# Attention of a decoder block on one core: q, k, probabilities and values from float32r pairs to float16 pairs, with wider spacing of the attention steps

## The chip, the cores and the metric

The kernel runs on one core of one Trainium2 chip. The metric is the device time of one execution in microseconds (us), from the launch on the device to its end; shorter is better. Times are medians over several executions.

The engines are named as in the profile: PE is TensorE (matrix products; PEld its weight loads), DVE is VectorE, ACT is ScalarE, POOL is GpSimd, SP is SyncE, whose queue issues most of the DMAs.

## The reference

One decoder block over 1024 tokens of width 1024. Attention and a causal convolution work on the same normalised input, are merged by sigmoid gates and projected; a SwiGLU feed-forward layer follows. The part that matters here is attention: three groups of 8 heads of width 64, with dilation 1, 4 and 16, each query attending at most 128 steps back, with a learned bias by distance.

```python
s = jnp.einsum('brnqhd,brnkhd->brnhqk', qb, kb).astype(jnp.float32) * (Dh ** -0.5) + bias
s = jnp.where(valid[:, None], s, NEG_INF)
lse = jax.nn.logsumexp(s, axis=-1)
p = jnp.exp(s - lse[..., None])
o = jnp.einsum('brnqhk,brnkhd->brnqhd', p, vb.astype(jnp.float32))
...
alpha = jax.nn.softmax(jnp.stack(lses, axis=0), axis=0)
o = jnp.einsum('gbsh,gbshd->bshd', alpha, jnp.stack(outs, axis=0))
```

All arrays are float32. The group outputs are merged with weights that come from their softmax denominators.

## The kernel before

**Products in two parts.** A float32 operand is carried as a high part in a short format and a low part that holds the rest. A product of two such operands is three products: high by high, high by low, low by high. Most of the kernel uses float16 parts, after a scaling of the weights by a power of two that is taken from their size (`self.scale`); attention, the output projections and the last layer use float32r parts.

**Stages.** In order: the first gate and convolution inputs; the remaining gates, convolution inputs and then q and k, in pairs of weight tiles by a Winograd scheme of seven products (`winograd`, lines 454 to 456), with the depthwise convolution on VectorE beside it; the value projection V (`v`, lines 1094 to 1098: products of 256 columns), with attention beside it; the gate and convolution-output units (`unit`, lines 438 to 442: products of 512 columns), into which attention runs on; the attention output, the mix projection and the feed-forward layer.

**q and k.** `qk_pair` writes each result to DRAM in two parts (`d_qk`), rows grouped by dilation. `stack_load` later brings them back for one pair of heads: `k` with its high rows over its low rows, and q as two tiles whose second halves GpSimd fills by copies (`double`, lines 1035 and 1036). So a score takes two products of full height (line 1192).

**Attention steps.** `attention` is a generator of 96 steps: 12 head pairs of 8 query blocks each. A step has one key block or two. At step s it emits: the scores of block s and, on VectorE, their sum with the bias and the row bound (`att_s`, lines 1192 and 1195); the exponential of block s - 1 on ScalarE (`att_e`, 1205); the transposes of block s - 3 and their two parts, the cast on ScalarE and the subtraction on VectorE (`att_t`, 1228, 1233, 1234); the products with the values of block s - 4, one of 128 and one of 64 columns per head and key block (`att_p`, 1249 and 1251), and a sum of their parts (1256). Loads for the next head pair are issued at its first steps, the bias tile (`bias_tile`, 613) as the fifth.

**Values.** Each V eviction (ScalarE, 1104 and 1106) writes float32 to DRAM (`d_v`); `values` loads a pair's values, and `value_parts` makes two parts of them on ScalarE and GpSimd (1069 and 1070) just before use.

**What sets the order.** All instructions are recorded in the order in which the Python code emits them, and each engine works through its own in that order. The generator is advanced by `beat`: each product of the V stage and of the units adds `RATE` to a credit (`RV` in the V stage, `RU` behind it), and a whole credit runs the generator to its next `yield`, three or four to a step. Other side work (`tick`, `later`, `bg`) hangs on counts of products too. So the numbers `RV` and `RU` say how many large products stand between two pieces of attention. Tiles come from rings of buffers (`half`: 11 tiles of 128x512 float32, named c; `slot`: b; `ring`: d), and whoever takes a buffer waits for its last reader.

Of the kernel before, what the change touches and what calls it, by code (L numbers as in the profile page):

```python
# [18 lines left out]
T = 1024  # L19
# [16 lines left out]
RV, RU = 0.42, 0.8  # L36
# [6 lines left out]
TINY, W_TOP, H_TOP = 2.0 ** -60, 2.0 ** -13, 256.0  # L43

# [25 lines left out]
class Build:  # L70
# [21 lines left out]
    def ring(self):  # L92
        self.uid += 1
        return self.pool.tile([128, 1024], F32, tag="d", bufs=NRING, name=f"d{self.uid}")
# [680 lines left out]
    def conv_consts(self):  # L775

        nc = self.nc
        self.nbu = self.small.tile([128, 8], F32, name="nbu")
# [169 lines left out]
    def qk_pair(self, g, hp, job):  # L948
# [3 lines left out]
        _, un, _, un8 = self.scale[job]  # L952
        dil = DILS[g]
# [17 lines left out]
        def parts(y, hf, dst, scale):  # L971
            h = self.half(F32R)
            nc.scalar.activation(h, y, AF.Copy, scale=scale)
            nc.vector.scalar_tensor_tensor(y.bitcast(F32R), y, scale, f(h), op0=OP.mult, op1=OP.subtract)

            def store():
                out(dst, 0, hf, f(h))
                out(dst, 1, hf, y)

            self.hold(store)  # L980

        def row1(hf):
            def g(z, x):
                y = self.half()
                nc.vector.tensor_tensor(perm(y), nat(z), nat(x), op=OP.add)
                return lambda: parts(y, hf, dk, un)
            return g

        def f22(x, v):
            y = self.half()  # L990
            nc.vector.tensor_tensor(perm(y), nat(x), nat(v), op=OP.add)
            return lambda: parts(y, 1, dq, un8)

        def f21(x):
            h, l = self.half(F32R), self.half(F32R)
            nc.scalar.activation(perm(h), nat(x), AF.Copy, scale=un8)
            nc.vector.scalar_tensor_tensor(perm(l), nat(x), un8, perm(f(h)), op0=OP.mult, op1=OP.subtract)

            def store():
                out(dq, 0, 0, f(h))  # L1000
                out(dq, 1, 0, f(l))

            self.hold(store)
# [8 lines left out]
    def stack_load(self, p, i):  # L1012
# [4 lines left out]
        if i < 2:  # L1017
            a, b = self.slot(F32R), self.slot(F32R)
            nc.sync.dma_start(f(a[top]), dq[i * 64:i * 64 + 64])
            nc.sync.dma_start(f(b[low]), dq[128 + i * 64:192 + i * 64])  # L1020
            p[2][i][1:] = a, b
        elif i < 4:
            k = self.slot(F32R)
            for part, rows in enumerate((top, low)):
                e = part * 128 + (i - 2) * 64
                nc.sync.dma_start(f(k[rows]), dk[e:e + 64])
# [4 lines left out]
    def double(self, p, hf):  # L1031

        s, top, low = slice(hf * H, (hf + 1) * H), slice(0, 64), slice(64, 128)
        for k, a, b in p[2]:
            self.nc.gpsimd.tensor_copy(a[low, s], f(a[top, s]))
            self.nc.gpsimd.tensor_copy(b[top, s], f(b[low, s]))
# [13 lines left out]
    def values(self, g, hp):  # L1050

        x = self.slot()
# [11 lines left out]
    def value_parts(self, x, i):  # L1064

# [1076 lines left out]
```

## Time and profile before

| | us |
|---|---|
| median of 3 runs | 1684.94 (1684.65 to 1686.24) |
| the profiled execution: its own time | 1684.47 |
| the profiled execution: span of its instructions | 1682.6 |
| TensorE busy in the span | 1644.7 |
| VectorE, ScalarE, GpSimd busy | 1275.8, 995.4, 468.0 |
| attention, first score to last product with values | 599 to 849 of the span |
| end of the V products | 782 |

In the profile a row of a group has the line, the engine, the operation, out<-in by the program's tile names, the shape and count, then busy us and the mean ns of one, then idle time before it and what ended it. In a timeline a row has start and duration in us. In windows a row has the busy us of each engine in a stretch of time, with the number of instructions, then the TensorE clock that was granted (1.00 is full), the share of the DMA engines and GB/s. In a list of waits a row has the total us, the number of times and the longest.

### The profile page before, as it was taken

Reading aid. Unit: us, or ns where it says so; the run is one execution under the profiler, and the core shown is the slowest. Engines: PE = TensorE matmul, PEld = TensorE weight load, DVE = VectorE, ACT = ScalarE, POOL = GpSimd, SP = SyncE. Lnnn points to the kernel's source line nnn. Section 1 sums busy time; section 2 is a strip of 40 time slices with the busy share of each in tenths; the row PEclk is TensorE's granted clock in tenths of the full one; section 3 lists DMA queues with packets and bytes.
Section 4 is the critical chain, followed back from the end, with each engine's and each line's share of the span. In section 5 each row is a group of like instructions: output and inputs, shape, how many; then the busy total and the mean of one; then the engine's idle time right before and its main releaser. Section 6 shows DMA issues by size and latency. Waiting matters only on the chain.

```text
span 1682.6 us, 25027 instructions
## 1 busy us (share of the span) xinstructions
PE 1644.7 (98%) x8757; PEld 1060.7 (63%) x8757; DVE 1275.8 (76%) x2467; ACT 995.4 (59%) x1875; POOL 468.0 (28%) x384
## 2 busy tenths in 40 slices
PE   8999999999999989999999999999999999999998
PEld 6744444444444979989788878544444444588886
DVE  6889999999998766697764856677667657677686
ACT  6476676666665777778622456755555555454453
POOL 0007777787775145646300110000000000000000
PEclk9999999999999999999999999999999999999999
DMA  4352343455567897978845732222322322494334
GB/s 168 126 191 88 125 150 132 149 185 198 175 172 202 246 278 219 248 206 250 267 175 190 278 112 72 75 107 102 138 99 94 130 96 94 154 377 126 107 126 156
DMA packets 159481, 277.06 MB, mean 165 GB/s; under 512 B 46993, under 2 KB 78412, under 8 KB 159356
## 3 DMA queue, kind: packets, MB, share of 16 engines
q1 hardware_dynamic: 155148, 263.30, 47.2%
q0 software_dynamic: 3920, 11.91, 2.3%
q8 instruction: 69, 1.13, 0.3%
q14 instruction: 56, 0.46, 0.1%
q10 hardware_dynamic: 288, 0.27, 0.0%
HBM read 184.81 MB, written 95.33 MB: 166 GB/s over the span
## 4 chain that ended last, share of the span: by engine, by line
PE 77%; DVE 9%; ACT 4%; POOL 3%; issue 3%; DMA 2%; DVEq 0%; SPq 0%; POOLq 0%; ACTq 0%
PE p L2026 12%; PE p L454 11%; PE p L456 11%; PE p L455 11%; PE p L1751 4%; PE p L438 4%; PE p L442 4%; PE p L440 4%; DVE p L833 3%; PE p L692 2%; PE p L1098 2%; PE p L1094 2%; PE p L1096 2%; PE p L1192 2%; PE p L1228 1%
## 5 line engine op out<-in xcount | busy, mean ns | idle before, releaser
L456 PE MATMUL p<-b,b 128*128 128x512 f16 x1032 | 391.1, 379 | 2.9 <-POOL b L294 2.9
L454 PE MATMUL p<-b,b 128*128 128x512 f16 x1032 | 391.0, 379 | 2.2 <-ACT c L468 1.6
L455 PE MATMUL p<-b,b 128*128 128x512 f16 x1032 | 391.0, 379 | 0.0
L2026 PE MATMUL p<-b,b 128*128 128x512 f32 x924 | 209.8, 389 | 0.0
L2026 PEld LDWEIGHTS p<-b,b 128*128 128x128 f32 x924 | 173.4, 188 | 36.1
L456 PEld LDWEIGHTS <-b 128*128 128x128 f16 x1032 | 100.8, 98 | 127.6 <-POOL b L294 6.6
L454 PEld LDWEIGHTS <-b 128*128 128x128 f16 x1032 | 100.9, 98 | 120.9
L455 PEld LDWEIGHTS <-b 128*128 128x128 f16 x1032 | 100.8, 98 | 119.5 <-issue 3.0
L833 DVE SCALAR_TENSOR_TENSOR p<-b,par,p 128x511 f32<-128x511 f32 (+14 forms) x232 | 163.9, 739 | 0.0
L438 PE MATMUL p<-b,b 128*128 128x512 f32 (+1 forms) x368 | 144.8, 393 | 1.5 <-ACT b L284 1.5
L442 PE MATMUL p<-b,b 128*128 128x512 f32 (+1 forms) x368 | 143.9, 391 | 0.4 <-DVE b L285 0.4
L440 PE MATMUL p<-b,b 128*128 128x512 f32 (+1 forms) x368 | 143.9, 391 | 0.0
L285 DVE SCALAR_TENSOR_TENSOR b<-d,sc,b 128x1024 f16<-128x1024 f32 x40 | 51.2, 1281 | 87.7 <-ACT b L284 87.7
L294 POOL TENSOR_TENSOR b<-d,b 128x1024 f16<-128x1024 f32 x44 | 96.1, 2184 | 74.7 <-ACT b L293 74.6
L1094 PE MATMUL p<-b,b 128*128 128x256 f16 x384 | 105.9, 276 | 0.1
L1096 PE MATMUL p<-b,b 128*128 128x256 f16 x384 | 106.0, 276 | 0.0
L1098 PE MATMUL p<-b,b 128*128 128x256 f16 x384 | 105.9, 276 | 0.0
L1344 DVE TENSOR_TENSOR b<-c,b 128x512 fp32r<-128x512 f32 (+1 forms) x101 | 70.1, 695 | 37.1 <-ACT b L1343 37.0
L1343 ACT CAST b<-b 128x512 fp32r<-128x512 f32 (+1 forms) x117 | 72.1, 617 | 42.9 <-PE p L2026 18.3
L1344 DVE TENSOR_TENSOR b<-b,b 128x512 fp32r<-128x512 f32 (+1 forms) x117 | 80.1, 688 | 19.7 <-ACT b L1343 18.2
L1751 PE MATMUL p<-b,b 128*128 128x512 f32 x384 | 90.1, 392 | 0.0
L1205 ACT ACTIVATE c<-c,stat 128x128 f32<-128x128 f32 (+1 forms) x192 | 84.8, 445 | 8.8 <-DVE stat L1195 8.7
(272 smaller groups left out, 3548.9 us busy)
## 6 DMA issues: line engine op xcount, KB each, us to landing
b<-w_in SPq DMA_DIRECT2D x30, 512.0 KB, 4.6
dk<-c SPq DMA_DIRECT2D x48, 256.0 KB, 2.5
dq<-c SPq DMA_DIRECT2D x48, 256.0 KB, 3.1
b<-dq SPq DMA_DIRECT2D x48, 256.0 KB, 8.6
b<-dk SPq DMA_DIRECT2D x48, 256.0 KB, 8.6
b<-w_fi SPq DMA_DIRECT2D x24, 512.0 KB, 5.2
d<-w_in SPq DMA_DIRECT2D x23, 512.0 KB, 4.8
dqS<-c SPq DMA_DIRECT2D x44, 256.0 KB, 2.0
```

What stands on the lines that cost most here:

```text
L438: nc.tensor.matmul(ps, hi[:, s], a, start=kt == 0, stop=False)
L440: nc.tensor.matmul(ps, hi[:, s], b, start=False, stop=False)
L442: nc.tensor.matmul(ps, lo[:, s], a, start=False, stop=kt == nk - 1)
L454: nc.tensor.matmul(ps, hi[:, s], a, start=first and kt == 0, stop=False, skip_group_check=True)
L455: nc.tensor.matmul(ps, hi[:, s], b, start=False, stop=False, skip_group_check=True)
L456: nc.tensor.matmul(ps, lo[:, s], a, start=False, stop=kt == 3, skip_group_check=True)
L833: nc.vector.scalar_tensor_tensor(A[i][:, j:], src[i][:, :H - j], w[i], A[i][:, j:], op0=OP.mult, op1=OP.add)
L1094: nc.tensor.matmul(o, a, hi[:, s], start=kt == 0, stop=False)
L1096: nc.tensor.matmul(o, a, lo[:, s], start=False, stop=False)
L1344: nc.vector.tensor_tensor(s[:, 512:512 + n], src, f(s[:, :n]), op=OP.subtract)
L1751: nc.tensor.matmul(banks[tt][nh], st, wt[:, nh * H:(nh + 1) * H], start=bool(kt == 0 and a), stop=bool(kt == KT - 1 and b))
L2026: nc.tensor.matmul(acc[t], x, y, start=first and e == 0, stop=last and e == 2, skip_group_check=True)
```

## The change

The attention operands become float16 pairs.

- `qk_pair` scales each q and k by `KEEP`, a fixed power of two, and writes high and low float16 parts; the factor that undoes it, with the weights' scale, is kept per head pair (`sig`) and multiplied in where scores and bias are added. For that the bias tile is divided by the same factor: `scale_bias`, a reciprocal on VectorE and a pass of ScalarE over the bias tile, emitted behind the seventh step of the pair before. `d_qk` is float16, so its stores and loads have half the bytes. Two operand tiles share one slot (`packed`).
- V evictions write the high part (ScalarE) and the low part (VectorE) directly, as float16 under `KEEP`; `d_v` holds both parts, with the same number of bytes as before. `value_parts` is gone: the loaded tile is used as it is.
- The probabilities' two parts are float16 under `P_TOP`, in one tile instead of two. The factors of values and probabilities are undone in the merge (`vun`).
- `RV` goes from 0.42 to 0.36, `RU` from 0.8 to 0.66.

```diff
-RV, RU = 0.42, 0.8
+RV, RU = 0.36, 0.66
...
+KEEP, P_TOP = 2.0 ** -12, 2.0 ** 14
...
-        def parts(y, hf, dst, scale):
-            h = self.half(F32R)
-            nc.scalar.activation(h, y, AF.Copy, scale=scale)
-            nc.vector.scalar_tensor_tensor(y.bitcast(F32R), y, scale, f(h), op0=OP.mult, op1=OP.subtract)
...
+        def parts(y, hf, dst):
+            x = self.half(F16, [128, T])
+            nc.scalar.activation(x[:, :H], y, AF.Copy, scale=KEEP)
+            nc.vector.scalar_tensor_tensor(x[:, H:], y, KEEP, x[:, :H], op0=OP.mult, op1=OP.subtract)
+            store(hf, dst, x)
...
-            a, b = self.slot(F32R), self.slot(F32R)
-            nc.sync.dma_start(f(a[top]), dq[i * 64:i * 64 + 64])
-            nc.sync.dma_start(f(b[low]), dq[128 + i * 64:192 + i * 64])
+            a, b = self.packed(), self.packed()
+            nc.sync.dma_start(a[top], dq[i * 64:i * 64 + 64])
+            nc.sync.dma_start(b[low], dq[128 + i * 64:192 + i * 64])
...
+    def scale_bias(self, p):
+        c = 4 * p[0] + p[1]
+        r = self.tiny(1, "rsig", 3)
+        self.nc.vector.reciprocal(r, self.sig[:, c:c + 1])
+        self.nc.scalar.activation(p[3], p[3], AF.Copy, scale=r)
...
-    def value_parts(self, x, i):
-
-        v = self.slot(F32R)
-        d = v.rearrange("p (t e c) -> p t e c", t=8, e=2)
-        y = x[:, i * H:(i + 1) * H].rearrange("p (t c) -> p t c", t=8)
-        self.nc.scalar.copy(d[:, :, 0], y)
-        self.nc.gpsimd.tensor_tensor(d[:, :, 1], y, f(d[:, :, 0]), op=OP.subtract)
-        return v
...
             if i % 4 == 0:
-                x = self.ring()
-                nc.scalar.activation(x[:, :H], ps, AF.Copy, scale=un)
-            else:
-                nc.scalar.activation(x[:, H:], ps, AF.Copy, scale=un)
+                x = self.ring(F16, [128, 2 * T])
+            y = x[:, i % 4 * H:i % 4 * H + T].rearrange("p (a e c) -> p a e c", e=2, c=64)
+            z = ps.rearrange("p (a c) -> p a c", c=64)
+            nc.scalar.activation(y[:, :, 0], z, AF.Copy, scale=KEEP)
+            nc.vector.scalar_tensor_tensor(y[:, :, 1], z, KEEP, y[:, :, 0], op0=OP.mult, op1=OP.subtract)
+            if i % 4:
                 self.later(2, lambda i=i, x=x: out(i, x))
                 x = None
...
+                if u == 7 and nxt:
+                    self.scale_bias(nxt)
...
-                                           bt[:, hh * 256 + 256 - n:(hh + 1) * 256], 1.0, 3e38, OP.add, OP.min,
+                                           bt[:, hh * 256 + 256 - n:(hh + 1) * 256], sig, 3e38, OP.add, OP.min,
...
-        hi, lo = self.half(F32R), self.half(F32R)
-        nc.scalar.copy(hi[:, :n], ps[:, :n])
-        nc.vector.tensor_tensor(lo[:, :n], ps[:, :n], f(hi[:, :n]), op=OP.subtract)
+        hi, lo = self.two(H)
+        nc.scalar.activation(hi[:, :n], ps[:, :n], AF.Copy, scale=P_TOP)
+        nc.vector.scalar_tensor_tensor(lo[:, :n], ps[:, :n], P_TOP, hi[:, :n], op0=OP.mult, op1=OP.subtract)
```

Two places in the order of the instructions are spoken of below. The first is on TensorE in the V stage, where a step's products with values stand between V products (names are out<-in: p is a bank, b and c tiles, the number a tile's). Before, for a head with two key blocks:

```order
L1228 MATMUL p_8012<-ident,c_7870 128x128 x4
L1094 LDWEIGHTS b_690
L1094 MATMUL p_7975<-b_7633,b_690 128x256
L1096 LDWEIGHTS b_690
L1096 MATMUL p_7975<-b_7633,b_690 128x256
L1249 MATMUL p_8023<-b_7873,c_7964 128x128
L1251 MATMUL p_8023<-b_7873,c_7965 128x64
L1249 MATMUL p_8023<-b_7873,c_7964 128x128
L1251 MATMUL p_8023<-b_7873,c_7965 128x64
L1098 LDWEIGHTS b_690
L1098 MATMUL p_7975<-b_7633,b_690 128x256
```

Now, for a head with one key block (the lines have shifted: 1248 and 1250 are the products with values, 1096 to 1100 those of V):

```order
L1248 LDWEIGHTS c_7128
L1248 MATMUL p_7187<-b_6645,c_7128 128x128
L1250 LDWEIGHTS c_7128
L1250 MATMUL p_7187<-b_6645,c_7128 128x64
L1098 LDWEIGHTS b_633
L1098 MATMUL p_7185<-b_6702,b_633 128x256
L1100 LDWEIGHTS b_633
L1100 MATMUL p_7185<-b_6702,b_633 128x256
L1096 LDWEIGHTS b_644
L1096 MATMUL p_7185<-b_6702,b_644 128x256
L1248 LDWEIGHTS c_7128
L1248 MATMUL p_7187<-b_6645,c_7128 128x128
```

The weight load of a float32r product is part of the product; that of a float16 product is an instruction of its own in front of it. Both parts of the probabilities now come from one tile.

The second place is on ScalarE, in the steps of one head pair with one key block. Before, with the casts of the values (1069) and a V eviction (1106) between exponentials (1205) and casts of the probabilities (1233):

```order
L1233 CAST c_7512<-p_7509 128x256
L1069 CAST b_7538<-b_7300 128x8x64
L1205 ACTIVATE c_7496,stat_7137<-c_7496,stat_7137 128x128 x2
L1233 CAST c_7551<-p_7548 128x256
L1106 ACTIVATE d_7368<-p_7370,sc_6745 128x512
L1069 CAST b_7585<-b_7300 128x8x64
```

Now, with the scaling of the bias tile of the next pair (1046) and a V eviction (1108):

```order
L1232 ACTIVATE c_7340<-p_7337 128x256
L1108 ACTIVATE d_7182<-p_7185 128x8x64
L1204 ACTIVATE c_7327,stat_6828<-c_7327,stat_6828 128x128 x2
L1232 ACTIVATE c_7383<-p_7380 128x256
L1046 ACTIVATE c_7330<-c_7330,rsig_7422 128x512
L1204 ACTIVATE c_7366,stat_6828<-c_7366,stat_6828 128x128 x2
L1232 ACTIVATE c_7432<-p_7429 128x256
```

The casts of the values are gone from ScalarE; a pass over a tile that a DMA brings (c_7330) stands between the exponentials instead.

More of the change, by code (lines that the diff above doesn't have):

```diff
@@ L1132, in attention @@
                         if x is None and there():
-                            x, wait = self.values(*nxt[:2]), 45
-                        elif x is not None and cur is None and not V:
-                            wait -= 1
-                            if wait < 0:
-                                V = [self.value_parts(x, i) for i in range(2)]
+                            x = self.values(*nxt[:2])
                         yield 0
@@ L1541, in build @@
     B.d_att = {(g, hp): B.dram.tile([T, 128], F32, name=f"datt{g}{hp}") for g in range(2) for hp in range(4)}
[L1542 removed]
+    B.d_v = {(g, hp): B.dram.tile([T, 256], F16, name=f"dv{g}{hp}") for g in range(3) for hp in range(4)}
     B.d_ot = [B.dram.tile([128, 1024], F32, name=f"dot{p}") for p in range(2)]
```

67 lines of the change are left out of this document (35 added, 32 removed).

## The prediction

> **What bounds the kernel now.** I read the page first, then the stage in which attention runs, by windows.
>
> ```profile
> PE 1644.7 (98%) x8757; PEld 1060.7 (63%) x8757; DVE 1275.8 (76%) x2467; ACT 995.4 (59%) x1875; POOL 468.0 (28%) x384
> ...
> PE 77%; DVE 9%; ACT 4%; POOL 3%; issue 3%; DMA 2%; DVEq 0%; SPq 0%; POOLq 0%; ACTq 0%
> ```
>
> TensorE is busy for 98% of the span and holds 77% of the chain that ended last. So an edit pays by the TensorE time that it takes out, unless another engine stops TensorE instead. The stage that the edit touches, cut where the value projection (V) ends:
>
> ```profile
> core 0: us, PE busy (x) PEld busy (x) DVE busy (x) ACT busy (x) POOL busy (x), PEclk, DMA share, GB/s
> 600.00:620.00 20.00, 15.26 (x126) 13.22 (x125) 13.14 (x46) 15.46 (x45) 7.55 (x11) 0.93 1.01 279
> 620.00:640.00 20.00, 20.00 (x171) 19.00 (x170) 12.04 (x42) 12.32 (x38) 9.51 (x13) 0.90 1.06 258
> 720.00:760.00 40.00, 38.47 (x352) 36.23 (x353) 36.94 (x112) 30.08 (x89) 22.13 (x26) 1.00 0.69 191
> 599.00:782.00 183.00, 175.58 (x1614) 165.72 (x1614) 135.55 (x484) 137.30 (x427) 95.11 (x124) 0.98 0.86 236
> 782.00:849.00 67.00, 62.93 (x429) 54.50 (x427) 46.72 (x169) 45.18 (x151) 25.07 (x31) 1.00 0.73 234
> ```
>
> The first score product stands at 599, the last product with values at 849: 250 us. TensorE is nearly full in both parts; VectorE and ScalarE are at three quarters (135.55 and 137.30 of 183 us). There is one hole, at 600 to 620 us, with a granted clock of 0.93 and then 0.90 behind it and DMA engines full.
>
> **The change, part by part.** The float32r products of attention become float16 products. Their counts:
>
> ```profile
> L1249 PE MATMUL p<-b,c 128*128 128x128 f32 x279 | 78.2, 305 | 2.4 <-DVE b L1256 1.0 <-DVE d L1256 0.8 <-ACT c L1233 0.6
> L1251 PE MATMUL p<-b,c 128*128 128x64 f32 x279 | 67.9, 250 | 3.4 <-DVE c L1234 2.9
> L1192 PE MATMUL p<-b,b 128*128 128x128 f32 x208 | 33.8, 282 | 4.9 <-DMA b<-dk 4.1 <-POOL b L1036 0.8
> L1192 PE MATMUL p<-b,b 128*128 128x256 f32 x176 | 32.2, 305 | 0.0
> ```
>
> (280 pairs in the program; one lies just past the window.) The durations overlap, so I price by starts: what a group of products adds between its float16 neighbours of 256 columns. TensorE's timeline, columns start and duration in us:
>
> ```profile
> 611.51 0.27 PE L1094 MATMUL p<-b,b 128*128 128x256 f16 x1
> 611.54 0.30 PE L1249 MATMUL p<-b,c 128*128 128x128 f32 x1
> 611.68 0.24 PE L1251 MATMUL p<-b,c 128*128 128x64 f32 x1
> 611.76 0.31 PE L1249 MATMUL p<-b,c 128*128 128x128 f32 x1
> 611.91 0.24 PE L1251 MATMUL p<-b,c 128*128 128x64 f32 x1
> 611.99 0.28 PE L1096 MATMUL p<-b,b 128*128 128x256 f16 x1
> 612.11 0.27 PE L1098 MATMUL p<-b,b 128*128 128x256 f16 x1
> 612.14 0.71 PE L1192 MATMUL p<-b,b 128*128 128x256 f32 x4
> 612.70 0.28 PE L1094 MATMUL p<-b,b 128*128 128x256 f16 x1
> ```
> ```profile
> 700.92 0.27 PE L1094 MATMUL p<-b,b 128*128 128x256 f16 x1
> ...
> 700.95 0.31 PE L1249 MATMUL p<-b,c 128*128 128x128 f32 x1
> ...
> 701.18 0.28 PE L1096 MATMUL p<-b,b 128*128 128x256 f16 x1
> ...
> 701.79 0.27 PE L1098 MATMUL p<-b,b 128*128 128x256 f16 x1
> ...
> 701.82 0.64 PE L1192 MATMUL p<-b,b 128*128 128x128 f32 x4
> ...
> 702.30 0.29 PE L1094 MATMUL p<-b,b 128*128 128x256 f16 x1
> ```
>
> Neighbours without a group between them start 0.109 us apart. Two pairs of value products take 0.48 - 0.11 = 0.37, one pair 0.26 - 0.11 = 0.15, four scores of 256 columns 0.59 - 0.11 = 0.48, four of 128 columns 0.51 - 0.11 = 0.40. With four scores a step, 176 and 208 of them are 44 steps with two key blocks and 52 with one; each does its value products once per head:
>
> - values now: 88 x 0.370 + 104 x 0.147 = 47.9 us;
> - scores now: 44 x 0.478 + 52 x 0.401 = 41.9 us.
>
> A float16 product of 128 or 64 columns does not occur in the trace. The lower bound is the column rate: 256 columns in 0.109 give 0.055 for 128 and 0.028 for 64. That holds only if the weight load hides, and these rows speak for it:
>
> ```profile
> 598.57 0.27 PE L1098 MATMUL p<-b,b 128*128 128x256 f16 x1
> 598.68 0.17 PE L144 MATMUL p<-pb,ones 128*128 128x1 bf16 x1
> 598.71 0.27 PE L1094 MATMUL p<-b,b 128*128 128x256 f16 x1
> 598.82 0.27 PE L1096 MATMUL p<-b,b 128*128 128x256 f16 x1
> ```
>
> A bf16 product of one column, with its own 128x128 weights, adds 0.03 us, and the next float16 product, whose weights had to be loaded beside it, is not late. So a 16-bit load takes at most 0.03 us of TensorE's pace. I take 0.056 and 0.029: values 280 x 0.085 = 23.8, scores 44 x 0.437 + 52 x 0.224 = 30.9. **TensorE saves 24.1 + 11.0 = 35 us.** The upper bound is a load that does not hide and costs its recorded time (`98` ns in the next row):
>
> ```profile
> L454 PEld LDWEIGHTS <-b 128*128 128x128 f16 x1032 | 100.9, 98 | 120.9
> ```
>
> Then values take 560 x 0.098 = 54.9 and scores 208 x 0.098 + 176 x 0.109 = 39.6: 5 us more than now. The one-column product is the nearer row, since it shows load and product together.
>
> The Trainium skill ("TensorE: Matmul & The Clock Gate", Back-to-back issue gap) gives a stream of load and product pairs about 81 ns each at 128 columns, against 56 ns for a product alone. By 81 ns for every short product the saving would be 8 us, not 35. The one-column row contradicts it in this trace.
>
> **Wider steps.** In the order of TensorE's instructions six steps take 57 V products before and 66 or 67 now, and 30 and 36 of the 512-column products that follow; attention ends 226 instead of 137 such products into the gate and convolution-output units. These products are only moved. Beside them merges of heads 2 and 3 move too, still ahead of the units that need them. Price 0 on TensorE.
>
> **VectorE, ScalarE, GpSimd.** Rows of 599 to 849 us:
>
> ```profile
> L1234 DVE TENSOR_TENSOR c<-p,c 128x512 fp32r<-128x512 f32 x44 | 30.4, 690 | 22.9 <-ACT c L1233 21.8 <-ACT b L1343 0.7
> L285 DVE SCALAR_TENSOR_TENSOR b<-b,sc,b 128x512 f16<-128x512 f32 x14 | 11.0, 789 | 1.0 <-ACT b L284 0.8 <-DMA b<-w_v 0.2
> ...
> L1069 ACT CAST b<-b 128x512 fp32r<-128x512 f32 x22 | 13.6, 619 | 0.0
> ...
> L1070 POOL TENSOR_TENSOR b<-b,b 128x512 fp32r<-128x512 f32 x22 | 29.7, 1350 | 67.0 <-ACT b L1069 33.9 <-issue 13.3 <-DMA c<-dact 7.0
> ```
>
> GpSimd loses 24 subtractions (30 us here), ScalarE 24 casts (-14 us) and gains 12 bias scalings of 128x512 (+8 us by the 0.62 to 0.72 us of such passes). VectorE gains 24 evictions of the low part, 14 of them in the V part of the stage: 14 x 0.74 = +10 us; its 96 subtractions for the probabilities become the three-operand form, which is up to 0.1 us longer (789 against 690 ns): +4 us there. With 66 steps in the V part instead of 72 (-8 us; a step's own VectorE rows come to about 1.4 us), VectorE has 135.6 + 10 + 4 - 8 = 142 us of work there. TensorE's own work there: 664 V products x 0.109 = 72.5, 37 steps of two blocks x (0.437 scores + 0.437 transposes + 0.340 values) = 44.9, 29 of one x 0.612 = 17.7, merges 1.7: **137 us**. VectorE becomes the longer of the two. It was busy 36.94 of 40 us at 720 to 760, with TensorE idle only 1.5 us, so 92% is possible: 142 / 0.92 = 154 us for the V part, against 183 now. In the tail TensorE has 226 x 0.216 = 48.8, with 7 steps of 1.214, 23 of 0.612 and some more of merges: 72 us; VectorE 46.7 + 8 for the six more steps = 55.
>
> **The sum.** TensorE's own work in the stage now: V 72.5, 137 x 0.216 = 29.6, transposes 32.3, values 47.9, scores 41.9: 224 of 250 us. 26 us are waits and slow starts: 14 in the V part, whose own work is 72.5 + 40 x 1.655 + 32 x 0.912 + 1.7 = 169 of 183 us (40 steps of two blocks, 32 of one, at the prices above), and 12 in the tail. After it I take 154 - 137 = 17 in the V part and the same 12 in the tail: 29, of which the q and k loads, halved, may give back some at 600 to 620 us. 35 - 3 = **32 us off the profiled execution**, 1684.47 (span 1682.6), 0.5 us under the median of the three runs: 1684.94 - 32 = **1653 us**. Ahead of the stage, in the q and k units, only types change: 0, give or take 4.
>
> **The rivals.** (1) *The waits shrink with the DMA.* The longest of them:
>
> ```profile
> PE p L1192 <- DMA b<-dk: 4.1, 3, 2.4
> ```
>
> q and k loads fall from 256 to 128 KB each. If the hole at 600 to 620 and its low clock (about 8 us together) go and no wait grows: 1684.9 - 35 - 8 = 1642, and 1636 if the 12 us of the tail halve too.
>
> (2) *VectorE's duty stays near 85%.* Casts, subtractions and reductions hang on each other step by step (L1234 waits 22.9 us for ScalarE). At 85% the V part takes 142 / 0.85 = 167, 13 more than in the sum: 1666 us. At the 74% of now it would be 192, and 1691 us, slower.
>
> (3) *The bias tile stops ScalarE.* Its scaling (L1046) stands in ScalarE's queue three steps' exponentials ahead of the next pair; exponentials, casts and V evictions queue behind it and TensorE waits for those after about one step, 2.4 us. Now only VectorE waits for that tile, later.
>
> ```profile
> DMA to landing us min/median/max: 3.3/7.0/10.7
> ```
> ```profile
> 773.85 0.59 SPq L613 DMA_DIRECT2D c<-rep  x1
> ```
> ```profile
> 775.33 0.51 ACT L1205 ACTIVATE c<-c,stat 128x256 f32<-128x256 f32 x1
> ```
>
> This load is issued 1.4 us ahead of the exponential before which the scaling will stand; at 610.9, 793.9 and 817.7 it is likewise within 2 us of that place or behind it, the other seven are 5 us or more ahead. Landing after 7 us, or 10.7 as the one at 793.9, the four would hold ScalarE 29 us and TensorE 29 - 4 x 2.4 = 19, of which 3 stand in the sum: 1669 us. Against it: with one probability tile instead of two the loads wait less for a free buffer.
>
> (4) *Slower: weight loads don't hide.* The place is the value products of 64 columns; the price is the 98 ns above, +5 us, and with the 3 us of waits 1693. It is slower from 92 ns per short product on (768 short products x 0.092 + 19.2 = the present 89.8 us). Only the recorded load durations speak for it; the one-column row speaks against it. By the Trainium skill's 81 ns (the section named above) the same mechanism would end at 1684.9 - 8 + 3 = 1680.
>
> **How the numbers follow.** Forecast (1645 to 1662) 57%; (1) 12%; (2) 14%, one of these at the duty of now and slower; (3) 9%; (4) 6%: a load that half hides leaves two of these faster, one the same and three slower; saving and waits in balance, so that nothing measurable is left, 2%. The forecast's bounds are the 4 us of the units ahead and waits of 25 to 35 us; the range of 1638 to 1670 takes in (1) to (3). A change of 0.2%, 3.4 us, is about what a measurement of this kernel can tell. So faster 57 + 12 + 13 + 9 + 2 = 0.93, the same 1 + 2 = 0.03, slower 1 + 3 = 0.04.
>
> **What would show it.** The two value products with starts about 0.085 us apart per pair, scores at 0.056 or 0.109; V part of the stage near 154 us with VectorE at 90% or more; no wait of ScalarE for `rep` beyond a few us. Wrong if short products start 0.08 us or more apart, if TensorE's idle time in the stage passes 35 us, or if it grows outside the stage.

## The result and the profile after

The changed kernel takes 1698.8 us (median of four runs, 1696.35 to 1699.49) against 1684.8 for the kernel before: a ratio of 1.0082 with an interval of 1.0064 to 1.0099, **14.0 us slower**. Predicted were 1653 us, 32 faster. The page of the changed kernel, whose profiled execution took 1698.31 us:

```profile
PE 1622.9 (96%) x8757; PEld 1008.6 (59%) x8757; DVE 1308.0 (77%) x2525; ACT 995.8 (59%) x1863; POOL 437.5 (26%) x360
...
PE 69%; DVE 13%; ACT 6%; POOL 5%; issue 4%; DMA 2%; SPq 0%; DVEq 0%; ACTq 0%; POOLq 0%
```

TensorE is busy for 21.8 us less (1644.7 before), so there was a gain. But it idles 36 us more, and the chain of waits has moved from TensorE (77% to 69%) to VectorE, ScalarE and GpSimd. The time was lost in front of TensorE.

To see where, I compared the start of the same product in both traces. Up to 405 us, when the q and k units begin to permute their rows by dilation, the changed kernel is 0.6 us late. At the first V product it is 10 us late (551.1 against 540.8), at the first score 15 (613.9 against 598.8), at the last product with values 34 (883.2 against 849.4). From 908 us on it is 13.9 late and stays so. The 34 and the 14 differ because 226 instead of 137 products of the tail lie ahead of the last product with values, 89 x 0.216 = 19 us of work that is only moved. So 15 us come from ahead of the stage, and in the stage itself nothing is won. The windows of the changed kernel (first the q and k units, then the V part and the tail of the stage):

```profile
core 0: us, PE busy (x) PEld busy (x) DVE busy (x) ACT busy (x) POOL busy (x), PEclk, DMA share, GB/s
400.00:540.00 140.00, 128.44 (x582) 56.11 (x581) 132.01 (x186) 92.92 (x123) 100.60 (x60) 0.99 0.42 109
613.00:780.00 167.00, 142.39 (x1475) 124.11 (x1475) 134.44 (x453) 117.08 (x363) 65.38 (x92) 0.96 0.61 182
780.00:884.00 104.00, 92.47 (x670) 62.72 (x668) 73.31 (x244) 62.97 (x208) 27.03 (x40) 0.97 0.66 199
```

and of the kernel before, its q and k units:

```profile
400.00:540.00 140.00, 134.71 (x625) 60.06 (x624) 134.73 (x194) 91.98 (x135) 103.89 (x62) 1.00 0.62 176
```

In the q and k units TensorE starts 43 products fewer in the same 140 us. VectorE is almost full there in both kernels. In the V part VectorE is busy for 134.44 of 167 us, 81%, where the prediction had 92%; TensorE has holes and a lower granted clock (0.96).

The stage's idle time, counted as in the prediction: own work of TensorE after is V 72.5, tail 48.8, transposes 32.3, values 23.8 and scores 30.9, 208 us, in 269.3 us of stage (613.9 to 883.2). So **61 us are waits**, against 26 before and 29 predicted.

The products themselves are as fast as forecast. TensorE's timeline of the changed kernel, a value pair of each of two key blocks and then four scores (1248 and 1250 are the products with values, 1190 the scores, 1096 to 1100 V):

```profile
663.71 0.27 PE L1098 MATMUL p<-b,b 128*128 128x256 f16 x1
663.82 0.22 PE L1248 MATMUL p<-b,c 128*128 128x128 f16 x1
663.87 0.19 PE L1250 MATMUL p<-b,c 128*128 128x64 f16 x1
663.90 0.22 PE L1248 MATMUL p<-b,c 128*128 128x128 f16 x1
663.96 0.19 PE L1250 MATMUL p<-b,c 128*128 128x64 f16 x1
663.99 0.27 PE L1100 MATMUL p<-b,b 128*128 128x256 f16 x1
664.10 0.27 PE L1096 MATMUL p<-b,b 128*128 128x256 f16 x1
664.21 0.60 PE L1190 MATMUL p<-b,b 128*128 128x256 f16 x4
664.64 0.27 PE L1098 MATMUL p<-b,b 128*128 128x256 f16 x1
```

Two pairs add 0.28 - 0.11 = 0.17 us and the four scores 0.54 - 0.11 = 0.43, the prices of the prediction. Four scores of 128 columns add 0.34 - 0.11 = 0.23 (at 702.30 us of the same timeline), as priced too. At these prices the 35 us of TensorE's own work were saved.

**What took them.** First the q and k units. The groups of the changed kernel at 400 to 550 us, the two passes that make the parts of one of q's two halves (function `f21` in `qk_pair`):

```profile
L1005 ACT ACTIVATE c<-p 128x512 f16<-128x512 f32 x7 | 17.2, 2459 | 0.0
L1006 DVE SCALAR_TENSOR_TENSOR c<-p,c 128x512 f16<-128x512 f32 x7 | 17.2, 2452 | 4.1 <-ACT c L1005 4.1
```

The same passes in the kernel before, at 400 to 540 us:

```profile
L996 ACT ACTIVATE c<-p,sc 128x512 fp32r<-128x512 f32 x7 | 8.0, 1145 | 0.0
L997 DVE SCALAR_TENSOR_TENSOR c<-p,sc,c 128x512 fp32r<-128x512 f32 x7 | 7.8, 1111 | 0.0
```

They read a bank in order and write with the row order permuted by dilation, so neighbouring elements land far apart. Written as float32r such a pass takes 1.1 us, as float16 2.45. In the four units of dilation 1, before 400 us, the same lines write without permuting: 0.67 and 0.74 us as float32r, 0.58 and 0.68 as float16. The distance between neighbours is not what decides. The kernel groups the rows by 4 at dilation 4 and by 8 at dilation 16 (every other step is masked there), so at 256 bytes apart float16 (by 4) takes 2.44 to 2.46 us and float32r (by 8) 1.10 to 1.15, in the timelines of the two kernels. One pass follows the other, and VectorE, which is full there, does the convolution between: 1.34 us more for each of its eight passes are 10.7 us, about what the first V product is late.

Next the stage. Waits of ScalarE at 610 to 885 us in the changed kernel (total us, times, longest):

```profile
ACT c L1232 <- PE p L1227: 31.4, 39, 1.7
ACT c L1046 <- DVE rsig L1045: 22.8, 11, 3.4
...
ACT b L1345 <- DMA c<-dact: 8.6, 2, 6.9
...
ACT c L1046 <- DMA c<-rep: 3.3, 1, 3.3
```

The scaling of the bias tile (L1046) waits 22.8 us, and for the tiny reciprocal (L1045), not for the tile's load. Why a 0.16 us instruction comes late is seen on VectorE's timeline:

```profile
649.20 0.69 DVE L1233 SCALAR_TENSOR_TENSOR c<-p,c 128x512 f16<-128x512 f32 x1 [0.53 <-ACT c L1232]
649.81 0.41 DVE L1255 TENSOR_REDUCE d<-p 128x128 f32<-128x256 f32 x1
650.17 0.48 DVE L1194 CUSTOM_DVE_ANT_0 c<-p,c,sig 128x256 f32<-128x256 f32 x1
...
650.98 0.16 DVE L1045 RECIPROCAL rsig<-sig 128x1 f32<-128x1 f32 x1
653.39 0.69 DVE L1233 SCALAR_TENSOR_TENSOR c<-p,c 128x512 f16<-128x512 f32 x1 [2.25 <-ACT c L1232]
```

and on ScalarE's of the same moment:

```profile
648.57 0.60 ACT L1232 ACTIVATE c<-p 128x512 f16<-128x512 f32 x1 [0.78 <-PE p L1227]
651.17 0.72 ACT L1046 ACTIVATE c<-c,rsig 128x512 f32<-128x512 f32 x1 [2.00 <-DVE rsig L1045]
...
652.78 0.57 ACT L1232 ACTIVATE c<-p 128x512 f16<-128x512 f32 x1
```

The reciprocal stands in VectorE's queue behind the whole step: behind the subtraction L1233, which waits for ScalarE's part L1232, a reduction (L1255) and two sums (L1194). ScalarE works in order and can pass nothing by it, so it stands for 2 us; then its next probability part is 4.2 us behind the last, and now VectorE stands 2.25 us for it. TensorE meets this in the products with values (waits of TensorE at 613 to 884 us, changed kernel):

```profile
PE p L1248 <- ACT c L1232: 12.3, 7, 4.6
PE p L1250 <- DVE c L1233: 11.8, 22, 0.9
```

The same two waits were 0.6 and 2.9 us before. Third, the sums of scores and bias take their factor from a tile now. Groups of the changed kernel at 613 to 884 us:

```profile
L1194 DVE CUSTOM_DVE_ANT_0 c<-p,c,sig 128x256 f32<-128x256 f32 x88 | 38.7, 476 | 1.0 <-PE p L1190 0.9
L1194 DVE CUSTOM_DVE_ANT_0 c<-p,c,sig 128x128 f32<-128x128 f32 x104 | 31.9, 343 | 3.2 <-PE p L1190 1.7 <-ACT c L1046 0.8
```

and before, at 599 to 849 us:

```profile
L1195 DVE CUSTOM_DVE_ANT_0 c<-p,c 128x256 f32<-128x256 f32 x88 | 33.4, 418 | 2.6 <-PE p L1192 2.5
L1195 DVE CUSTOM_DVE_ANT_0 c<-p,c 128x128 f32<-128x128 f32 x104 | 25.8, 286 | 11.6 <-PE p L1192 7.1 <-DMA c<-rep 4.1 <-DMA b<-dk 0.2
```

57 or 58 ns more each, 11 us in all (70.6 against 59.2). These are three suspects, and the wider spacing is a fourth. All the experiments compute the whole block.

### The profile page after: what moved, and what is told of

It is laid out like the page before. It is cut to its first block, busy times and chain, and to the rows that moved or that the text cites. A ratio compares the mean times of both kernels' runs of the same rounds, so it can differ in the third digit from the quotient of the medians.

```text
span 1696.5 us, 24859 instructions
## 1 busy us (share of the span) xinstructions
PE 1622.9 (96%) x8757; PEld 1008.6 (59%) x8757; DVE 1308.0 (77%) x2525; ACT 995.8 (59%) x1863; POOL 437.5 (26%) x360
## 3 DMA queue, kind: packets, MB, share of 16 engines
q1 hardware_dynamic: 155148, 238.13, 41.4%
q8 instruction: 68, 1.11, 0.3%
## 4 chain that ended last, share of the span: by engine, by line
PE 69%; DVE 13%; ACT 6%; POOL 5%; issue 4%; DMA 2%; SPq 0%; DVEq 0%; ACTq 0%; POOLq 0%
PE p L2028 12%; PE p L456 11%; PE p L458 11%; PE p L457 11%; PE p L1753 4%; PE p L442 4%; PE p L440 4%; PE p L444 4%; DVE p L837 2%; POOL b L296 2%; DVE c L1194 1%; ACT junk L131 1%; PE p L1190 1%; DVE c L1233 1%; PE p L1096 1%
## 5 line engine op out<-in xcount | busy, mean ns | idle before, releaser
L2028 PE MATMUL p<-b,b 128*128 128x512 f32 x924 | 209.8, 390 | 0.0
L440 PE MATMUL p<-b,b 128*128 128x512 f32 (+1 forms) x368 | 147.5, 401 | 1.5 <-ACT b L286 1.5
L444 PE MATMUL p<-b,b 128*128 128x512 f32 (+1 forms) x368 | 146.1, 397 | 0.4 <-DVE b L287 0.4
L442 PE MATMUL p<-b,b 128*128 128x512 f32 (+1 forms) x368 | 145.7, 396 | 0.0
L1345 ACT CAST b<-c 128x512 fp32r<-128x512 f32 (+1 forms) x101 | 62.1, 616 | 52.7 <-DMA c<-dqA 17.3
```

The source lines that it names most:

```text
L440: nc.tensor.matmul(ps, hi[:, s], a, start=kt == 0, stop=False)
L442: nc.tensor.matmul(ps, hi[:, s], b, start=False, stop=False)
L444: nc.tensor.matmul(ps, lo[:, s], a, start=False, stop=kt == nk - 1)
L1345: nc.scalar.copy(s[:, :n], src)
L2028: nc.tensor.matmul(acc[t], x, y, start=first and e == 0, stop=last and e == 2, skip_group_check=True)
```

## The experiments

Differences are taken to the kernel before, run beside each one on the same chip (its medians lay between 1684.8 and 1686.8), as differences of medians; the last column is that less 14.0. The intervals are 2 to 3 us wide to either side, so differences of that size between two rows say little.

| kernel | us | ratio (interval) | to before | to the changed kernel |
|---|---|---|---|---|
| the change | 1698.8 | 1.0082 (1.0064 to 1.0099) | +14.0 | |
| reciprocal early | 1685.52 | 0.9993 (0.9981 to 1.0005) | -1.3 | -15.3 |
| permuted on the read side | 1685.27 | 0.9996 (0.9986 to 1.0006) | -1.5 | -15.5 |
| true scale | 1676.25 | 0.994 (0.9925 to 0.9955) | -10.6 | -24.6 |
| kernel before, spacing only | 1697.36 | 1.0065 (1.0049 to 1.0081) | +10.6 | -3.4 |
| the change, old spacing | 1708.33 | 1.013 (1.0115 to 1.0145) | +22.7 | +8.7 |
| reciprocal early and read side | 1669.82 | 0.9898 (0.9884 to 0.9912) | -16.1 | -30.1 |
| true scale and read side | 1658.25 | 0.9836 (0.9821 to 0.985) | -27.4 | -41.4 |
| ... with the old spacing | 1654.14 | 0.9811 (0.9794 to 0.9827) | -31.5 | -45.5 |
| ... and all blocks read-side | 1654.58 | 0.9813 (0.9799 to 0.9828) | -31.0 | -45.0 |
| true scale, read side, loads five ahead | 1653.91 | 0.9807 (0.9794 to 0.9821) | -32.0 | -46.0 |
| ... with RV 0.36, RU 0.8, loads three ahead | 1656.0 | 0.9821 (0.9808 to 0.9834) | -29.9 | -43.9 |
| ... with the old spacing, loads five ahead | 1654.42 | 0.9814 (0.98 to 0.9827) | -31.5 | -45.5 |

### Reciprocal early

The reciprocals of all twelve head pairs are taken in the q and k units, where their input is made, and kept; nothing else changes.

```diff
 nc.vector.tensor_scalar(self.sig[:, c:c + 1], un8, un, KEEP ** -2, op0=OP.mult, op1=OP.mult)
+nc.vector.reciprocal(self.rsig[:, c:c + 1], self.sig[:, c:c + 1])
...
-        r = self.tiny(1, "rsig", 3)
-        self.nc.vector.reciprocal(r, self.sig[:, c:c + 1])
-        self.nc.scalar.activation(p[3], p[3], AF.Copy, scale=r)
+        self.nc.scalar.activation(p[3], p[3], AF.Copy, scale=self.rsig[:, c:c + 1])
```

> The changed kernel, with one thing moved: the reciprocal of a head pair's factor is taken in its q and k unit instead of beside the scaling of its bias tile, so ScalarE's scaling waits for no VectorE instruction. In the profile of the changed kernel that scaling waited 22.8 us for the reciprocal (11 times), and TensorE waited 12.3 us for ScalarE's probability parts and 11.8 us for VectorE's. Theory A (these waits pass through to TensorE): 12 to 20 us less than the changed kernel, 1679 to 1687 us, and the first of TensorE's two waits below 5 us. Theory B (VectorE simply has too much work in the stage): under 4 us less, and the waits only change their names.

Twelve instructions of 0.16 us, put elsewhere in VectorE's queue, are worth 15 us. The wait for `rsig` is gone from ScalarE's list. TensorE's two main waits in the stage of this kernel:

```profile
PE p L1250 <- DVE c L1233: 9.6, 14, 1.5
PE p L1248 <- ACT c L1232: 9.6, 4, 5.7
```

The time is that of theory A, but the first wait was to fall below 5 us and fell only from 12.3 to 9.6. The gain is spread over TensorE's waits of the stage, which come to 28 us in its list instead of 37. Stage and idle time shrink by 12 us (257.3 and 49 us) in the profiled execution, which took 1687.69, 10.6 less than that of the changed kernel. So the late reciprocal is shown as a cause, with a size of 11 to 15 us, depending on how it is counted.

### Permuted on the read side

The same two passes of `f21` read the bank permuted and write in order.

```diff
-nc.scalar.activation(perm(h[:, :H]), nat(x), AF.Copy, scale=KEEP)
-nc.vector.scalar_tensor_tensor(perm(h[:, H:]), nat(x), KEEP, perm(h[:, :H]), op0=OP.mult, op1=OP.subtract)
+nc.scalar.activation(flat(h[:, :H]), by_class(x), AF.Copy, scale=KEEP)
+nc.vector.scalar_tensor_tensor(flat(h[:, H:]), by_class(x), KEEP, flat(h[:, :H]), op0=OP.mult, op1=OP.subtract)
```

> The changed kernel, with one block of q (of four blocks of q and k per head pair) permuted on the side that is read (float32 in its bank) instead of the side that is written (float16 in the tile), so the float16 parts are written without a stride. In the changed kernel the two passes take 2.45 us each at dilations 4 and 8, where the float32r ones took 1.11 to 1.14 us, and the q and k units of these dilations fall 9.8 us behind. Theory C (the strided float16 writes cause that): both passes under 1.2 us, 8 to 11 us less than the changed kernel, 1688 to 1691 us. Rival (the units fall behind for something else, such as shorter stores): under 3 us less.

Groups of this kernel at 400 to 550 us, and its window of the q and k units:

```profile
L1011 ACT ACTIVATE c<-p 128x512 f16<-128x512 f32 x8 | 4.6, 581 | 0.0
L1012 DVE SCALAR_TENSOR_TENSOR c<-p,c 128x512 f16<-128x512 f32 x8 | 5.4, 679 | 0.0
```
```profile
400.00:540.00 140.00, 135.59 (x630) 60.66 (x629) 134.66 (x202) 87.28 (x136) 103.87 (x62) 1.00 0.48 123
```

0.58 and 0.68 us instead of 2.45, as long as the unpermuted passes of dilation 1: the permuted read of a bank is free, the permuted float16 write is not. The lateness in the q and k units is gone, and the gain of 15.5 is more than the 8 to 11 that I expected. The first V product stands at 540.3 (before the change 540.8, after it 551.1) and the first score at 600.3 (598.8 and 613.9), so 3 of the 5 us that were lost between the two came back as well. The stage itself is as long as in the changed kernel (270.7 and 269.3). Why a strided 2-byte write is so slow stays open.

### True scale

q and k are scaled by the weights' own factors, as before the change, and stored as float16 of their true size. So there is no `sig`, no reciprocal and no pass over the bias, and the sums have the constant factor 1.0 again.

```diff
-        def parts(y, hf, dst):
+        def parts(y, hf, dst, w):
...
-            nc.scalar.activation(x[:, :H], y, AF.Copy, scale=KEEP)
+            nc.scalar.activation(x[:, :H], y, AF.Copy, scale=w)
...
-                return lambda: parts(y, hf, dk)
+                return lambda: parts(y, hf, dk, un)
...
-                if u == 7 and nxt:
-                    self.scale_bias(nxt)
...
-                     bt[:, hh * 256 + 256 - n:(hh + 1) * 256], sig, 3e38, OP.add, OP.min,
+                     bt[:, hh * 256 + 256 - n:(hh + 1) * 256], 1.0, 3e38, OP.add, OP.min,
```

> The changed kernel, with q and k parts scaled by the weights' own factors, as the kernel before did, instead of by a fixed power of two. So the factor per head pair is 1: no reciprocal, no scaling of the bias tile on ScalarE (12 passes of 0.72 us), and the sum with the bias on VectorE takes its factor as a constant (in the changed kernel, with the factor from a tile, 343 and 476 ns against 286 and 418 before, 11 us over 192 of them). Theory A: the 12 to 20 us of the early reciprocal, and little more, 1676 to 1687 us. Theory B (VectorE's work bounds the stage): 11 us from the shorter sums and the rest only from ScalarE's passes, so clearly better than the early reciprocal, by 8 us or more. If both passes return to 286 and 418 ns, the factor from a tile is what lengthened them.

24.6 us less than the changed kernel, 9.3 less than with the early reciprocal. So ScalarE's twelve passes (8.7 us by L1046 x12 at 722 ns) and the 11 us of longer sums cost something too. The sums, in the groups of this kernel:

```profile
L1188 DVE CUSTOM_DVE_ANT_0 c<-p,c 128x256 f32<-128x256 f32 x88 | 33.5, 417 | 1.7 <-PE p L1185 1.7
L1188 DVE CUSTOM_DVE_ANT_0 c<-p,c 128x128 f32<-128x128 f32 x104 | 25.7, 285 | 2.7 <-PE p L1185 1.7
```

back at the durations of before. These two costs are not told apart here.

### Spacing alone, on the kernel before

```diff
-RV, RU = 0.42, 0.8
+RV, RU = 0.36, 0.66
```

> The kernel before, with only the two spacing numbers of the change (0.36 and 0.66). The prediction priced the wider steps at 0. If that holds: 1685 us, within 3 us. Rival (wider steps cost, since attention and the merges end later and the last merges press on the units behind): 5 to 15 us more, with TensorE idle behind 850 us.

10.6 us slower: the price of 0 falls. The size is the rival's, the place is not: TensorE is busy throughout from 840 to 960 us. The V part is unharmed (175.61 us of TensorE's work in 183, before 175.58). The loss is at 800 to 840 us. ScalarE's wait there and the windows, first of this kernel, then of the kernel before:

```profile
ACT b L1343 <- DMA c<-dact: 18.2, 5, 8.0
```
```profile
800.00:820.00 20.00, 15.97 (x84) 13.76 (x83) 12.35 (x33) 9.54 (x28) 9.20 (x12) 0.83 1.04 236
820.00:840.00 20.00, 14.15 (x73) 12.18 (x71) 7.90 (x28) 6.58 (x23) 2.33 (x3) 0.74 0.77 177
```
```profile
800.00:820.00 20.00, 16.93 (x116) 14.55 (x116) 12.03 (x43) 12.71 (x41) 6.76 (x8) 1.00 0.87 249
820.00:840.00 20.00, 19.01 (x124) 16.46 (x123) 16.09 (x63) 14.11 (x53) 6.74 (x8) 1.00 0.84 302
```

The units load the convolution's output (`dact`) three tiles ahead. The loads of the last head pairs are issued among them in both kernels. With the wider spacing the DMA share at 800 to 820 us is 1.04 (0.87 before), the slowest `dact` load takes 14.1 us from issue to landing (8.5 before), and ScalarE's cast (L1343) waits up to 8.0 us for a `dact` tile. The probability parts of attention stand behind that cast. The wait was 5.3 us in four before. For this kernel the cause is read from its waits; no run of it has the loads issued earlier.

### The change with the old spacing

The reverse edit, on the changed kernel.

> The changed kernel with the two spacing numbers of the kernel before (0.42 and 0.8). The spacing alone, on the kernel before, cost 10.6 us: at 800 to 840 us ScalarE's queue stood behind casts that waited for the loads of the convolution's output, 12.7 us from issue to landing. Theory D (the wider steps push the last head pairs' loads into those loads, here too): 8 to 12 us less than the changed kernel, 1687 to 1691 us, with the clock between 800 and 840 us back at 1.00. Rival (with products this much shorter VectorE and ScalarE need the wider steps): within 3 us of the changed kernel or slower, with more waits of TensorE for the probability parts.

8.7 us slower, not faster: undoing the wider spacing on the changed kernel makes it worse, though its wait for `dact` is all but gone (1.0 us against 8.6). Theory D fails here, its clock too (0.89 and 0.85 at 800 to 840 us, not 1.00), and the rival's outcome is there: slower, with more waits for the probability parts. What ScalarE waits for instead, and TensorE's main wait:

```profile
ACT c L1046 <- DVE rsig L1045: 23.2, 10, 3.8
...
ACT c L1046 <- DMA c<-rep: 16.6, 2, 8.4
```
```profile
PE p L1248 <- ACT c L1232: 25.8, 12, 7.5
```

With steps closer together the scaling of the bias also comes ahead of its load (16.6 us against 3.3); TensorE's wait for the probability parts was 12.3 us. So one price for the spacing does not serve: what it costs depends on which load or tiny instruction it brings too near.

### The suspects together

Four kernels: true scale with the read side; the same with the old spacing; that one with the other three blocks of q and k permuted on the read side as well (their sums, lines 994 and 1000, read a tile and a bank by class and write in order); and, to part the scaling's costs, the early reciprocal with the read side.

> The changed kernel with two of the edits together: parts of q and k scaled by the weights' own factors (no factor per head pair, no reciprocal, no scaling of the bias tile), and the fourth block of q permuted on the side that is read. They gave 22.6 and 13.5 us one by one. If they are two places: 34 to 37 us less than the changed kernel, 1662 to 1665 us. If one lateness feeds the other (a late stage start was partly made good inside the stage): 25 to 30 us, 1669 to 1674 us.

> The same two edits, and the spacing of the kernel before. If the wider steps cost what they cost on the kernel before: 10 us less than with the wider steps, near 1653 us, which is the predicted time (35 us of TensorE saved and nothing given back). If the wider steps are needed once the rest is mended: the same or slower than with them, and TensorE's waits for the probability parts grow.

> As the run before it (two edits and the old spacing), with the other three blocks of q and k permuted on the read side too. In the changed kernel their three sums on VectorE write float32 with a stride and take 1.05 us each, in units where VectorE is busy 19 us of 20; with the stride on the read side the fourth block's passes fell from 2.45 to 0.58 and 0.68 us. If the same holds for two operands, one in a bank and one in a tile: 0.7 us each, 3 x 0.35 x 8 pairs = 8 us of VectorE less and, as far as TensorE waits for VectorE there (about 5 us), 2 to 5 us less. If a strided read of a tile costs what the strided write did: the same time.

> The changed kernel with the reciprocal taken early and the fourth block of q permuted on the read side; the fixed power of two stays, and with it ScalarE's 12 passes over the bias tiles (8.7 us) and the factor from a tile in VectorE's sums (11 us). With the weights' own factors instead of both, 1658.3 us. If the reciprocal's wait was all that mattered (theory A): the same within 3 us. If VectorE's and ScalarE's work counts as well (theory B): 8 to 14 us more, 1666 to 1672 us.

True scale and read side give 41.4 us together, alone 24.6 and 15.5: by the table they add up within 1.3 us, one lying ahead of the stage and the other in it. (The expectation counted from the plain medians, 22.6 and 13.5. By that count they give 40.6 together, above both of its ranges.) With the old spacing 4.1 more, not the 10 that it costs on the kernel before: 1654.14 us, 1 from the time predicted for the change. TensorE's waits for the probability parts hardly change (8.7 and 0.8 us against 7.6 and 3.9), so the wide steps are not needed there. The q and k units of the kernel with the old spacing, and its V part (599.8 to 759.3):

```profile
400.00:540.00 140.00, 136.32 (x635) 61.24 (x634) 134.47 (x196) 90.06 (x137) 104.14 (x62) 1.00 0.50 124
599.50:759.50 160.00, 146.29 (x1624) 130.93 (x1623) 140.10 (x505) 127.85 (x411) 71.85 (x105) 1.00 0.73 209
```

VectorE is busy for 88% of the V part, and the granted clock is 1.00. The stage has 219.1 us with 189 of own work, 30 of waits.

The other three blocks give nothing (-31.0 against -31.5). The sum of a tile and a bank takes as long when it reads with a stride as when it writes float32 with one. In the changed kernel's timeline such a sum takes 0.67 to 0.71 us unpermuted (dilation 1) and 1.02 to 1.07 written permuted. The group of them here, read permuted:

```profile
L998 DVE TENSOR_TENSOR c<-p,c 128x512 f32<-128x512 f32 x15 | 16.2, 1083 | 0.0
```

With the early reciprocal in place of the true scale, both with the read side and the wide spacing, the kernel takes 1669.82, 11.3 us more by the differences. That is theory B's range. So the passes over the bias and the longer sums together cost 11 us of time (and 9.3 without the read side, above), out of 20 us of work on two engines.

### The loads in the tail

```diff
-        x = [load(i) for i in range(3)]
+        x = [load(i) for i in range(5)]
...
-            if i < 13:
-                x.append(load(i + 3))
+            if i < 11:
+                x.append(load(i + 5))
```

This on "true scale and read side" with wide spacing; a spacing wide in the V part and old behind it, without it; and the old spacing with it.

> The two edits together with the wide steps (1658.3 us), and the loads of the convolution's output for its parts kept five ahead of their casts instead of three. There ScalarE still waited 7.0 us for these loads at 780 to 800 us, TensorE 3.6 us behind it at a clock of 0.83. Theory D (these loads land late among the last head pairs' loads and hold ScalarE's queue): 4 to 7 us less, 1651 to 1654 us, with no such wait above 2 us. If the loads are late because the DMA engines are full and not because they are issued late: the same time.

> The two edits with the wide steps in the V stage (0.36) and the old spacing behind it (0.8). If the wide steps lose only behind the V stage: as good as the old spacing throughout (1654.1 us) or up to 4 us better. If what decides is where the loads of the convolution's output fall, which stand in the V stage's last part: between 1654 and 1659 us.

> The two edits with the old spacing (1654.1 us) and the loads five ahead. In that kernel TensorE hardly waits for a ScalarE that waits for these loads. So: the same time within 2 us; if 3 us or more are gained, the late loads cost more there than its waits show.

With five tiles ahead the wide spacing comes down to the old one's time (1653.91 and 1654.42 against 1654.14), and with the old spacing five ahead changes nothing. The window that differs, first with three ahead, then with five:

```profile
780.00:800.00 20.00, 15.89 (x102) 10.90 (x100) 13.64 (x42) 11.71 (x36) 8.30 (x11) 0.83 0.98 278
```
```profile
780.00:800.00 20.00, 19.81 (x148) 13.66 (x147) 16.89 (x60) 14.38 (x47) 8.75 (x12) 1.00 1.01 242
```

ScalarE's wait for `dact` in the stage falls from 7.4 us to 0.6. So the 4 us of the spacing are the late `dact` tiles: 4 us of TensorE's time and a clock of 0.83 in that window, with nearly the same DMA share, so the loads were issued too late and not held up by full DMA engines alone. Closing the steps only behind V (1656.0, runs from 1654.7 to 1658.0) gains 2.5 us of it; that fits the second case of its expectation better than the first. On the kernel before, with its larger tiles, deeper loads were not tried.

## Why the prediction was wrong, point by point

**The sign fell on costs that the prediction set to nothing.** Between the 1653 predicted and the 1699 measured lie 46 us. Taken out one after the other, from the changed kernel on: permuted writes 15.5, late reciprocal 14.6 more, passes over the bias and longer sums 11.3, late loads under wider spacing 4.6. That comes to the whole of it within the noise of some 3 us, and the kernel without the four takes 1653.91. That this is so near 1653 is in part luck, as the fourth point shows.

- *TensorE saves 35 us.* Right. Pairs add 0.085 us and four scores 0.43 or 0.23, and the rival with weight loads that don't hide (98 ns) is out. The step from the one-column product to these held. The Trainium skill's 81 ns for a load and a product of 128 columns ("TensorE: Matmul & The Clock Gate", Back-to-back issue gap) does not hold in this trace: in the rows of the changed kernel's timeline above, the next product starts 0.05 to 0.06 us after one of 128 columns and 0.03 after one of 64.
- *"Ahead of the stage, in the q and k units, only types change: 0, give or take 4."* This step failed. I took a change of type at the same number of elements for no change of duration. But these passes write with a stride, and there the type decides: 2.45 us instead of 1.11 to 1.15. The trace of before showed the stride's cost already (1.11 to 1.15 us where the same lines at dilation 1 take 0.67 and 0.74), in units where VectorE is 96% busy. A longer pass there had no cover, and the prediction's "4" had no row behind it. TensorE came 10 us late to the first V product, and undoing the writes alone gave 15.5.
- *Waits of 29 us in the stage.* This failed too; it was 61, past the prediction's own limit of 35. With the reciprocal early it is 49. The reciprocal stood in no list of costs. Rival 3 had the right place (the scaling in ScalarE's queue, exponentials and parts behind it) and the wrong thing waited for: 3.3 us for `rep`, 22.8 for the reciprocal. I had looked at what feeds the tile by DMA and not at the queue in which the other input is made.
- *VectorE's work in the V part, 142 us at 92%, so 154 us.* Wrong in its parts. The list lacked 57 ns for each of the 192 sums, 11 us over the stage; the 4 us for three-operand subtractions were not there (L1233 takes 687 ns against 690 before); and 63 steps fall into the V part (35 with two key blocks, 28 with one), not 66. In the changed kernel VectorE has 134 us of work there, not 142, its duty is 81%, and the part takes 166 us. In the kernel with loads five ahead, which has the wide steps too, it is 126 us of 149, 84%, and the tail takes 90 us instead of 84. So VectorE at 92% is not what set this part, even with the mistakes undone. The stage still comes to 239 us against 238 in the sum because the two parts miss in opposite directions: that agreement is luck. Rival 2 named a duty of 85% and 167 us for the part; its time was nearer, with more work at a higher duty than there was.
- *The 8 us that ScalarE gets for the bias.* The duration is right (12 passes, 8.7 us). The estimate left open what it costs in time: with the longer sums it is 9 to 11 us.
- *Wider steps, price 0.* This failed. On the kernel before they cost 10.6 us, by its waits because the load of the next tile for another piece of work (`dact`) then lands late and holds ScalarE's queue. On the changed kernel the price has the other sign (8.7 us better than the old spacing). With the other mistakes undone it is 4, and nothing once those loads are issued earlier. I had counted products that move, and not the loads that move with the steps.
- *Rival 1, shorter waits with half the DMA bytes.* The wait for `dk` (4.1 us) is gone from TensorE's list in the stage; what it gave cannot be told from the rest.

The fastest version, true scale and read side with loads five ahead, beats both kernels: 1653.91 us, 0.9807 of the kernel before. The three with the old spacing are within 0.7 us of it.

## What to carry to other kernels

Price a pass by the stride and the element size of its write, not by its element count; where an engine is full, move a permutation to the read of a bank. For a tiny instruction ask whose queue it stands in, what is ahead of it, and which engine stands behind it: 0.16 us held another engine for 2 us on average. When a rate that spaces side work is changed, list the loads that move with it and whose buffers and queues they pass.

## What the runs showed of the hardware that I had not expected

- A 128x512 pass from a bank that writes float16 in permuted order takes 2.45 us on ScalarE as on VectorE; writing float32r so, 1.11 to 1.15; writing float16 in order, 0.58 and 0.68, whether the bank is read in order or permuted. At the same 256 bytes between neighbours float16 takes 2.45 us and float32r 1.14, so the element and not the distance decides. A permuted read of a tile beside the bank (VectorE's sum of the two) is not free: 1.07 to 1.08 us against 0.67 to 0.71 in order.
- A factor from a tile instead of a constant makes VectorE's fused sum and reduction 57 to 58 ns longer, at 128 columns (286 to 343 ns) as at 256 (418 to 476).
- In windows of 20 us in which TensorE idled 4.0 to 5.9 us, the granted clock was lower: 0.83 and 0.74 with spacing alone (4.0 and 5.9 us idle), 0.83 with true scale and read side (4.1), against 1.00 in the same stretch with loads five ahead (0.2). With 3.1 us idle at 800 to 820 us the kernel before had 1.00. So a wait may be paid with something on top; how much of the loss that is was not measured.
